# Another order of the seven block products in a feed-forward layer, a later place for half of the down-weight maxima, and two operand passes exchanged

## The chip, the cores and the metric
One core of one Trainium2 chip runs the kernel. The metric is device microseconds (us) of one execution, the median of several. TensorE (PE) does the matrix products, VectorE (DVE), ScalarE (ACT) and GpSimd (POOL) the elementwise work, and SyncE (SP) issues nearly all DMA transfers. Each engine works through its own instructions strictly in order and waits on semaphores for the others.

## The reference, cut to what matters
One layer over 2048 rows of 1024 float32 columns: four token mixers, an output projection with a norm, and a feed-forward part with 4096 hidden columns. The change lies in the last three steps:

```python
mix = jnp.concatenate([ya, yb, yc, yd], axis=-1)            # four mixers, 256 columns each
h = h + rms_norm(jnp.einsum('bsm,md->bsd', mix, w_out[layer]), norm_mix_post[layer])

u = rms_norm(h, norm_ffn_pre[layer])
f = jnp.square(jax.nn.relu(jnp.einsum('bsd,df->bsf', u, w_ff_up[layer])))
h = h + rms_norm(jnp.einsum('bsf,fd->bsd', f, w_ff_down[layer]), norm_ffn_post[layer])
```

## The kernel before
**What is multiplied.** The feed-forward products are Strassen-Winograd products of 2x2 blocks: seven products (indices 0 to 6) of sums and differences of blocks in place of eight. For accuracy each float32 operand is split into an f16 high part (a cast on ACT) and an f16 low part (a subtraction on DVE), and every product is done with three matmuls (`mm3`). The tuple `TURN` says in which order operands are made (`in_turn`), `SHELF` in which order f operands lie in DRAM.

**The up stage.** `ffn_norm` (L1593) loads rows of h (`nh`), normalises them, forms the four block differences `nt` on GpSimd with `diffs`, transposes all seven operands on PE (`fut`) and splits them into `u`. Then follow 32 blocks, `up_block(g, cp)` (L1705), for 16 pairs g of weight tiles and two halves cp of the rows. A block has seven products of 12 matmuls each. Its four PSUM accumulators X, Y, Z, V come from two rings of two banks. X takes product 0 and then 1, Y takes 5, Z takes 6 and then 3, V takes 4 and then 2. The second product of a bank is added onto the first one after DVE has read that first one: `us` is X (copied by ACT) plus Y, `c` is `us` plus Z, `c` then gets V added, and after products 3 and 2 there are further sums `c`. ACT takes relu and square of each into the tiles `e`.

`up_weights(g)` loads two raw weight tiles (`ur`), multiplies them by the norm gain on POOL, takes maxima on DVE (`a_up`, `m_up`), transposes the maxima on PE (`p_up`, in the code `p2_up`) for a scale `s_up`, forms differences `us0` to `us3` of weights on POOL and splits into `uw`. It runs two pairs ahead of the products. The names us80 to us83 are such weight differences, us60 and us61 the row sums of blocks (6,0) and (6,1).

**From up to down.** The results f of a block go to DRAM tiles `fD`. The 16 pairs are cut into six passes (`PASSES`, of 2, 2, 3, 3, 3, 3 pairs). For passes 1 to 5 `up_operands` (L1759) makes the sums `fz` on POOL and the splits `fs` at once and stores all seven operands in f16. For pass 0 `put` stores the raw float32 values, and `f_operands` (L1791) loads them in the down stage (`fr`), makes the sums `ft` on POOL and the splits `fo`.

**The down stage.** `run` (L1894) takes the passes in the order `QS` (1, 0, 2, 3, 4, 5). For each pass `down_weights` loads raw weights (`dr`), makes differences (`ds0..3`) on POOL and splits (`dw`), and eight calls of `down_block` (L1812) do seven products of 6 matmuls (passes of two pairs) or 9 matmuls each. They have the same four accumulators; the sums go into `y`, three of them on POOL (`y<-y,ds`). Before that, `down_top(x)` (L1686) has loaded the same raw weights once to take their maxima (`a_dn`) for the scale `kd`.

**The buffers that matter.** `ur` and `dr` tiles share one ring of two buffers (tag wraw): a load waits until the one before the last has been read for the last time. The down weights' temporaries and the block sum share the name `ds`.

**What sets the order.** Nearly every instruction is issued from L562 of a planner (`weave`) which merges lanes of work by due times, priorities and estimated costs into one static order for each engine. The order in which code is written inside a lane is kept. A `claim` takes a buffer early.

## Time and profile before

| what | value |
|---|---|
| median of three executions | 2643.15 us (2639.71 to 2643.21) |
| the profiled execution | 2652.18 us |
| its span in the trace | 2650.4 us |
| PE busy | 2460.2 us, 93% |
| DVE busy | 1801.0 us, 68% |
| ACT busy, POOL busy | 1261.8 us, 1180.5 us |
| mean granted PE clock | 0.971 |

In the profiled execution the out-projection ends and `ffn_norm` begins around 1200 to 1310 us, the steady up blocks run from 1431.4 to 1994.5, the down stage follows and its second pass (the raw one) lies from 2107.3 to 2201.5. A window's "PE busy" counts matmuls that run; what is missing to the window's length is time in which PE stood still. The clock column is a share of full speed.

### The profile page before, as it was taken

Reading aid. Unit: us, or ns where it says so; the run is one execution under the profiler, and the core shown is the slowest. Engines: PE = TensorE matmul, PEld = TensorE weight load, DVE = VectorE, ACT = ScalarE, POOL = GpSimd, SP = SyncE. Lnnn points to the kernel's source line nnn. Section 1 sums busy time; section 2 is a strip of 40 time slices with the busy share of each in tenths; the row PEclk is TensorE's granted clock in tenths of the full one; section 3 lists DMA queues with packets and bytes.
Section 4 is the critical chain, followed back from the end, with each engine's and each line's share of the span. In section 5 each row is a group of like instructions: output and inputs, shape, how many; then the busy total and the mean of one; then the engine's idle time right before and its main releaser. Section 6 shows DMA issues by size and latency. Waiting matters only on the chain.

```text
span 2650.4 us, 39473 instructions
## 1 busy us (share of the span) xinstructions
PE 2460.2 (93%) x14186; PEld 1299.4 (49%) x14186; DVE 1801.0 (68%) x3801; ACT 1261.8 (48%) x2563; POOL 1180.5 (45%) x1147
## 2 busy tenths in 40 slices
PE   7999999999989998987897999999997989999998
PEld 5545575656645565643444444444443434444443
DVE  6487986766788778657754677777756785445355
ACT  6377775434456676644334565565555321112022
POOL 5373331020265445444344545545534474344357
PEclk9999999999999997998897999999998999999999
DMA  6522226362351525237652333443335313333256
GB/s 185 151 72 83 83 74 186 70 182 46 87 150 50 154 83 157 85 89 244 223 164 80 96 115 115 129 129 111 124 116 193 128 48 136 120 136 135 103 190 221
DMA packets 306548, 334.33 MB, mean 126 GB/s; under 512 B 51316, under 2 KB 264244, under 8 KB 301743
## 3 DMA queue, kind: packets, MB, share of 16 engines
q1 hardware_dynamic: 306351, 331.79, 40.4%
q8 instruction: 112, 1.84, 0.3%
q14 instruction: 85, 0.70, 0.1%
HBM read 225.49 MB, written 113.06 MB: 128 GB/s over the span
## 4 chain that ended last, share of the span: by engine, by line
PE 52%; DVE 16%; POOL 10%; DMA 8%; ACT 7%; issue 6%; SPq 1%; DVEq 0%; POOLq 0%; ACTq 0%
PE mz L562 8%; PE mx L562 7%; PE mv L562 7%; PE pt L562 5%; PE po L562 4%; PE my L562 4%; DVE e L562 4%; POOL fz L562 3%; PE pv L562 2%; PE as L562 2%; ACT e L562 2%; PE do L562 2%; POOL y L562 2%; DVE fs L562 2%; PE dt L562 2%
## 5 line engine op out<-in xcount | busy, mean ns | idle before, releaser
L562 PEld LDWEIGHTS <-fo 128*128 128x128 f16 x2688 | 264.5, 98 | 362.7 <-issue 47.8
L562 PEld LDWEIGHTS <-uw 128*128 128x128 f16 x2688 | 264.3, 98 | 344.9 <-issue 39.2
L562 PE MATMUL pt<-uuh,wh 128*128 128x512 f16 x640 | 243.9, 381 | 0.1
L562 PE MATMUL pt<-uuh,wl 128*128 128x512 f16 x640 | 243.4, 380 | 0.5 <-DVE wl L562 0.5
L562 PE MATMUL pt<-uul,wh 128*128 128x512 f16 x640 | 243.5, 380 | 0.0
L562 POOL TENSOR_TENSOR y<-y,ds 128x512 f32<-128x512 f32 x112 | 147.2, 1338 | 206.9 <-DVE ds L562 206.9
L562 DVE CUSTOM_DVE_ANT_0 e<-sc,strip,scf 128x512 f32<-128x512 f32 (+3 forms) x320 | 206.1, 663 | 25.5 <-PE sc L562 16.0
L562 PE MATMUL mz<-dw,fo 128*128 128x512 f16 x768 | 185.1, 385 | 16.6 <-DVE y L562 16.3
L562 PE MATMUL mv<-u,uw 128*128 128x512 f16 x768 | 179.9, 383 | 21.9 <-DVE c L562 21.9
L562 PE MATMUL mx<-dw,fo 128*128 128x512 f16 x768 | 184.0, 381 | 16.3 <-ACT ds L562 11.7
L562 ACT ACTIVATE e<-e,dmn 128x1024 f32<-128x1024 f32 (+4 forms) x192 | 171.5, 895 | 47.3 <-DVE dmn L562 44.1
L562 PE MATMUL mv<-dw,fo 128*128 128x512 f16 x768 | 183.8, 383 | 3.1 <-DVE y L562 3.0
L562 PE MATMUL po<-woh,mx 128*128 128x512 f16 x512 | 169.2, 398 | 17.8 <-ACT mx L562 10.0
L562 PEld LDWEIGHTS <-wh 128*128 128x128 f16 x1280 | 123.1, 98 | 126.8 <-issue 22.5
L562 PE MATMUL mz<-u,uw 128*128 128x512 f16 x768 | 179.6, 380 | 3.1 <-DVE c L562 3.1
L562 PE MATMUL mx<-u,uw 128*128 128x512 f16 x768 | 180.8, 382 | 0.0
L562 POOL TENSOR_SCALAR e<-e,dcf 128x256 f32<-128x256 f32 (+4 forms) x96 | 77.4, 806 | 161.3 <-DVE dcf L562 127.5
L562 ACT ACTIVATE ae<-ae,mt 128x256 f32<-128x256 f32 (+1 forms) x192 | 87.1, 455 | 113.4 <-DVE mt L562 99.2
L562 POOL TENSOR_TENSOR ur<-ur,g_ffn 128x1024 f32<-128x1024 f32 x32 | 62.0, 1938 | 164.5 <-DMA ur<-in_w_ff_up_dram 151.0
L562 PEld LDWEIGHTS <-mx 128*128 128x128 f16 x768 | 77.4, 103 | 110.9 <-issue 13.7
L562 DVE TENSOR_TENSOR fs<-fz,fs 128x512 f16<-128x512 f32 x112 | 108.1, 1025 | 32.4 <-ACT fs L562 32.1
L562 ACT ACTIVATE ds<-mx 128x512 f32<-128x512 f32 x48 | 28.4, 591 | 202.0 <-PE mx L562 202.0
(332 smaller groups left out, 5626.1 us busy)
## 6 DMA issues: line engine op xcount, KB each, us to landing
fD<-fs SPq DMA_DIRECT2D x84, 512.0 KB, 3.0
fo<-fD SPq DMA_DIRECT2D x32, 1344.0 KB, 6.1
dr<-in_w_ff_down_dram SPq DMA_DIRECT2D x64, 512.0 KB, 4.5
ur<-in_w_ff_up_dram SPq DMA_DIRECT2D x32, 512.0 KB, 4.2
wr<-in_w_in_dram SPq DMA_DIRECT2D x24, 512.0 KB
xt<-in_x_dram SPq DMA_DIRECT2D x16, 512.0 KB, 8.0
mr<-mixT SPq DMA_DIRECT2D x16, 512.0 KB, 5.7
oxr<-in_x_dram SPq DMA_DIRECT2D x16, 512.0 KB, 4.8
```

Source lines behind the costliest of these rows:

```text
L562: op.ins.append(fn(*[real(a) for a in args], **{n: real(a) for n, a in kw.items()}))
```

## The change
There are seven edits.

1. `TURN` is (0, 5, 6, 4, 1, 3, 2), so operands are made in another order.
2. In `up_block` products run as X0, Y5, Z6, V4, X1, Z3, V2, where it was X0, Y5, X1, Z6, V4, Z3, V2. The first two blocks keep X1 before Z6. The tiles `e` are taken in the other order, and the choice between two pools for them switches from the third block on and not from the fifth.
3. `down_block` has the same new product order.
4. `QS` is (1, 2, 0, 3, 4, 5): the raw pass comes third.
5. In pass 0 only the half cp = 0 stays raw; cp = 1 is stored as ready f16 operands.
6. `ffn_norm` makes its differences on VectorE.
7. `down_top` is called for 8 of 16 pairs at the place where all 16 were; the others follow one per pair, for pairs 3 to 10 of the up weights.

```diff
@@ -31,8 +31,8 @@
 NC = -(-NB // 3)
 U = 1024.0
 UF = 256.0
-TURN = (0, 5, 1, 6, 4, 3, 2)
-QS = (1, 0, 2, 3, 4, 5)
+TURN = (0, 5, 6, 4, 1, 3, 2)
+QS = (1, 2, 0, 3, 4, 5)
 SHELF = (0, 1, 3, 2, 4, 5, 6)
 PASSES = ((0, 2), (2, 4), (4, 7), (7, 10), (10, 13), (13, 16))
 EPS = 1e-6
@@ -1605,7 +1605,7 @@
                 h.append(x)
             q = h[0][:, 0:512], h[1][:, 0:512], h[0][:, 512:D], h[1][:, 512:D]
             z = [np.tile([P, 512], F32, tag=f"at{i % 2}", name=f"nt{cp}{j}{i}")[:] for i in range(4)]
-            diffs(nc.gpsimd, *q, *z)
+            diffs(nc.vector, *q, *z)
         with nc.lane("fn", 0):
             for i, src in in_turn(*q, *z, True):
                 nc.claim(*u[i])
@@ -1633,8 +1633,8 @@
         self.k0 = k.keep.tile([P, self.pairs], F32, tag="k0", name="k0")
         self.kd = k.keep.tile([P, self.pairs], F32, tag="kd", name="kd")
 
-        self.f = [[k.dram.tile([4, P, p1 - p0, 7, 2, P] if q else [4, P, 2 * (p1 - p0), 2 * P], F16 if q else F32,
-                               tag=f"fD{q}{cp}", name=f"fD{q}{cp}") for cp in range(2)]
+        self.f = [[k.dram.tile([4, P, p1 - p0, 7, 2, P] if q + cp else [4, P, 2 * (p1 - p0), 2 * P],
+                               F16 if q + cp else F32, tag=f"fD{q}{cp}", name=f"fD{q}{cp}") for cp in range(2)]
                   for q, (p0, p1) in enumerate(PASSES)]
         self.w, self.d, self.n, self.made = {}, {}, 0, 0
 
@@ -1725,7 +1725,7 @@
 
         def put(f):
             x = 2 * (g - PASSES[q][0]) + f
-            if q == 0:
+            if q + cp == 0:
                 nc.sync.dma_start(self.f[q][cp][:, :, x, :].rearrange("j p c -> p j c"),
                                   e[f][:].rearrange("p j a t -> p j (a t)"))
         q = next(i for i, (p0, p1) in enumerate(PASSES) if p0 <= g < p1)
@@ -1734,26 +1734,32 @@
             nc.need(*u[TURN[-1]])
             s = k.fuw.tile([P, 512], F32, tag="s", name=f"us{g}{cp}", bufs=1)
             self.made += 1
-            er = self.fst if self.made > 4 and self.made % 2 else k.fuw
-            e = [er.tile([P, 4, 2, P], F32, tag="er", name=f"e{g}{cp}{f}", bufs=2) for f in range(2)]
+            er = self.fst if self.made > 2 and self.made % 2 else k.fuw
+            early = self.made <= 2
+            e = {f: er.tile([P, 4, 2, P], F32, tag="er", name=f"e{g}{cp}{f}", bufs=2) for f in ((0, 1) if early else (1, 0))}
+            if not early:
+                nc.claim(Z)
             prod(X, 0, True)
             nc.scalar.activation(s[:], X, AF.Copy)
             prod(Y, 5, True)
             nc.vector.tensor_tensor(s[:], s[:], Y, op=ALU.add)
-            prod(X, 1, False)
-            act(X, 0, 0)
-            prod(Z, 6, True)
-            c = add(Z)
-            prod(V, 4, True)
-            nc.vector.tensor_tensor(c[:], c[:], V, op=ALU.add)
-            act(c[:], 1, 1)
+            for step in (0, 1) if early else (1, 0):
+                if step:
+                    prod(Z, 6, True)
+                    c = add(Z)
+                    prod(V, 4, True)
+                    nc.vector.tensor_tensor(c[:], c[:], V, op=ALU.add)
+                    act(c[:], 1, 1)
+                else:
+                    prod(X, 1, False)
+                    act(X, 0, 0)
             prod(Z, 3, False)
             act(add(Z)[:], 1, 0)
             put(1)
             prod(V, 2, False)
             act(add(V)[:], 0, 1)
             put(0)
-        if q:
+        if q + cp:
             self.up_operands(q, g - PASSES[q][0], cp, e)
 
     def up_operands(self, q, x, cp, e):
@@ -1793,7 +1799,7 @@
         k, nc = self.k, self.k.nc
         n = PASSES[q][1] - PASSES[q][0]
         with nc.lane("fprep", 1):
-            if q:
+            if q + cp:
                 w = k.fdr.tile([P, n, 7, 2, P], F16, tag="fo", name=f"fo{q}{cp}{j}", bufs=2)
                 nc.sync.dma_start(w[:].rearrange("p n i h t -> p (n i h t)"),
                                   self.f[q][cp][j].rearrange("p n i h t -> p (n i h t)"))
@@ -1832,6 +1838,7 @@
                 nc.claim(y[ta], y[tb])
             X, Y, Z, V = self.banks(True)
             s = k.fue.tile([P, 512], F32, tag="s", name=f"ds{q}{cp}{j}", bufs=2)[:]
+            nc.claim(Z)
             prod(X, 0, True)
             nc.scalar.activation(s, X, AF.Copy)
             prod(Y, 5, True)
@@ -1839,15 +1846,15 @@
             if not first:
                 for o in (y22, y21, y12):
                     (nc.gpsimd if not last or o is not y12 else nc.vector).tensor_tensor(o, o, s, op=ALU.add)
+            prod(Z, 6, True)
+            add(y22, s if first else y22, Z)
+            prod(V, 4, True)
+            add(y22, y22, V)
             prod(X, 1, False)
             if not first:
                 add(y11, y11, X)
             else:
                 nc.scalar.activation(y11, X, AF.Copy)
-            prod(Z, 6, True)
-            add(y22, s if first else y22, Z)
-            prod(V, 4, True)
-            add(y22, y22, V)
             prod(Z, 3, False)
             add(y21, s if first else y21, Z)
             prod(V, 2, False)
@@ -1902,9 +1909,8 @@
             while ready < min(n, g + 2):
                 self.up_weights(ready, 1)
                 ready += 1
-                if ready == 2:
-                    for x in range(n):
-                        self.down_top(x)
+                for x in range(8) if ready == 2 else (ready + 5,) if 2 < ready < 11 else ():
+                    self.down_top(x)
             self.up_block(g, cp)
         self.down_scale()
         self.y = [k.fd.tile([P, D], F32, tag=f"y{t}", name=f"y{t}") for t in range(NT)]
```

Three places of the static order show what comes of it.

VectorE in block (6,0) of the up stage, before, from the sum with Y to the sum with product 3 (`a_up8` and `m_up8` are maxima of the up weights two pairs ahead, `mz`, `mv`, `my` the accumulators):

```order
L562 TENSOR_TENSOR us60_17867<-us60_17867,my_17858 128x512
L562 TENSOR_REDUCE a_up8_17871<-ur81_17833 128x1
L562 TENSOR_REDUCE m_up8_17910<-a_up8_17871 128x1
L562 TENSOR_TENSOR c60_17927<-us60_17867,mz_17899 128x512
L562 TENSOR_TENSOR fs2112_17844<-fz2113_17916,fs2112_17844 128x4x128
L562 TENSOR_TENSOR fs2114_17933<-fz2110_17873,fs2114_17933 128x4x128
L562 TENSOR_TENSOR fs2114_17933<-fz2111_17893,fs2114_17933 128x4x128
L562 TENSOR_TENSOR fs2116_17946<-fz2112_17905,fs2116_17946 128x4x128
L562 TENSOR_TENSOR c60_17927<-c60_17927,mv_17921 128x512
L562 TENSOR_REDUCE s_up8_17969<-p2_up8_17960 128x1
L562 TENSOR_SCALAR s_up8_17969<-s_up8_17969 128x1 x4
L562 TENSOR_TENSOR c60_17984<-us60_17867,mz_17899 128x512
```

After, the same place:

```order
L562 TENSOR_TENSOR us60_17899<-us60_17899,my_17894 128x512
L562 TENSOR_TENSOR kd_14591<-a_dn13_17878 128x1
L562 TENSOR_TENSOR c60_17943<-us60_17899,mz_17866 128x512
L562 TENSOR_TENSOR fs2112_17880<-fz2113_17934,fs2112_17880 128x4x128
L562 TENSOR_TENSOR fs2114_17950<-fz2110_17902,fs2114_17950 128x4x128
L562 TENSOR_TENSOR fs2114_17950<-fz2111_17914,fs2114_17950 128x4x128
L562 TENSOR_TENSOR fs2116_17961<-fz2112_17925,fs2116_17961 128x4x128
L562 TENSOR_REDUCE a_up8_17974<-ur80_17890 128x1
L562 TENSOR_TENSOR c60_17943<-c60_17943,mv_17939 128x512
L562 TENSOR_REDUCE a_up8_17974<-ur81_17923 128x1
L562 TENSOR_REDUCE m_up8_18001<-a_up8_17974 128x1
L562 TENSOR_TENSOR c60_18014<-us60_17899,mz_17866 128x512
```

Both maxima stood ahead of the sum with Z and now come behind the four splits, one of them ahead of the sum with V; the maximum's scale `s_up8` leaves this block for the next.

SP's DMA issues of the same pair, before (`fD` are stores of f operands):

```order
L562 DMA fD20_17362<-fs2104_17743 128x4x512
L562 DMA fD20_17362<-fs2106_17754 128x4x256
L562 DMA ur80_17783<-in_w_ff_up_dram 128x8x128
L562 DMA ur81_17833<-in_w_ff_up_dram 128x8x128
L562 DMA fD21_17529<-fs2110_17800 128x4x512
L562 DMA fD21_17529<-fs2112_17844 128x4x512
L562 DMA fD21_17529<-fs2114_17933 128x4x512
L562 DMA fD21_17529<-fs2116_17946 128x4x256
L562 DMA fD20_17362<-fs2200_17989 128x4x512
```

After:

```order
L562 DMA dr130_17838<-in_w_ff_down_dram 128x1024
L562 DMA dr131_17863<-in_w_ff_down_dram 128x1024
L562 DMA ur80_17890<-in_w_ff_up_dram 128x8x128
L562 DMA fD21_17562<-fs2110_17851 128x4x512
L562 DMA ur81_17923<-in_w_ff_up_dram 128x8x128
L562 DMA fD21_17562<-fs2112_17880 128x4x512
L562 DMA fD21_17562<-fs2114_17950 128x4x512
L562 DMA fD21_17562<-fs2116_17961 128x4x256
L562 DMA fD20_17392<-fs2200_18016 128x4x512
```

The two loads of raw down weights now go ahead of the two of up weights through the same two buffers.

GpSimd at the passage from up to down, before, from the last sum of block (15,1):

```order
L562 TENSOR_TENSOR fz5213_20948<-e1511_20871,fz5211_20931 128x512
L562 TENSOR_TENSOR ft000_21032<-fr000_20978 128x256
L562 TENSOR_TENSOR ft000_21042<-ft000_21032,fr000_20978 128x256
L562 TENSOR_TENSOR ds30_21048<-dr30_20993 128x512
L562 TENSOR_TENSOR ft000_21061<-fr000_20978 128x256
L562 TENSOR_TENSOR ds31_21067<-dr31_21020,ds30_21048 128x512
L562 TENSOR_TENSOR ds32_21078<-dr31_21020,dr30_20993 128x512
L562 TENSOR_TENSOR ds33_21088<-dr31_21020,ds31_21067 128x512
L562 TENSOR_TENSOR ft000_21107<-fr000_20978,ft000_21042 128x256
L562 TENSOR_TENSOR ds00_21136<-dr00_21096 128x512
L562 TENSOR_TENSOR ds01_21164<-dr01_21144,ds00_21136 128x512
L562 TENSOR_TENSOR fz5200_21166<-e1500_21012,e1501_21059 128x512
```

After:

```order
L562 TENSOR_TENSOR fz5213_21005<-e1511_20913,fz5211_20988 128x512
L562 TENSOR_TENSOR ds30_21084<-dr30_21038 128x512
L562 TENSOR_TENSOR ds31_21108<-dr31_21073,ds30_21084 128x512
L562 TENSOR_TENSOR ds32_21117<-dr31_21073,dr30_21038 128x512
L562 TENSOR_TENSOR ds33_21128<-dr31_21073,ds31_21108 128x512
L562 TENSOR_TENSOR ds40_21178<-dr40_21138 128x512
L562 TENSOR_TENSOR ds41_21209<-dr41_21188,ds40_21178 128x512
L562 TENSOR_TENSOR fz5200_21212<-e1500_21130,e1501_21115 128x512
L562 TENSOR_TENSOR ds42_21214<-dr41_21188,dr40_21138 128x512
L562 TENSOR_TENSOR fz5201_21216<-fz5200_21212,e1500_21130 128x512
L562 TENSOR_TENSOR fz5202_21218<-e1500_21130 128x512
L562 TENSOR_TENSOR fz5203_21220<-e1501_21115,fz5201_21216 128x512
```

The raw operand's sums `ft000` are gone from here, and the weights of pair 4 stand where those of pair 0 were.

On PE a steady block before was cut by the next one: X0, Y5, X1, Z6, V4, three matmuls of the next block's X0, Z3, V2, and the rest of that X0. After, each block is unbroken. The passes run 1, 2, 0, 3, 4, 5; the sums `ft` are made for four blocks of pass 0 where they were made for eight. The transposes `p_up` of the pair two ahead stood in the middle of Z3 of block (g,0); now they stand behind nine matmuls of X0 of block (g,1) for pairs 7 to 10, and in Z3 of (g,0) from pair 11 on.

## Rows read from the trace of the kernel before

**Rows 1.** The page: busy time, share and instructions of each engine, and one DMA group.
```profile
PE 2460.2 (93%) x14186; PEld 1299.4 (49%) x14186; DVE 1801.0 (68%) x3801; ACT 1261.8 (48%) x2563; POOL 1180.5 (45%) x1147
...
dr<-in_w_ff_down_dram SPq DMA_DIRECT2D x64, 512.0 KB, 4.5
```

**Rows 2.** Windows: start:end, length, busy time (instructions) by engine, PE clock, DMA share, GB/s.
```profile
1200.00:1250.00 50.00, 37.45 (x173) 18.75 (x172) 34.80 (x51) 18.33 (x31) 22.48 (x24) 0.86 0.75 254
1400.00:1450.00 50.00, 36.66 (x165) 21.36 (x163) 22.81 (x31) 24.78 (x44) 20.62 (x23) 0.73 0.21 64
1750.00:1800.00 50.00, 46.85 (x218) 21.39 (x217) 37.20 (x51) 26.28 (x45) 31.62 (x22) 1.00 0.34 110
2000.00:2050.00 50.00, 33.96 (x139) 14.18 (x137) 34.52 (x45) 24.66 (x42) 23.08 (x19) 0.83 0.59 203
2107.30:2201.50 94.20, 78.22 (x337) 33.83 (x336) 81.11 (x112) 29.52 (x73) 65.61 (x57) 0.95 0.21 65
2201.50:2295.70 94.20, 94.20 (x438) 42.78 (x437) 37.17 (x52) 8.37 (x14) 36.21 (x29) 1.00 0.33 120
```

**Rows 3.** Waits, stretch 1440 to 1990: engine <- releaser: us in total, times, longest.
```profile
PE mv L562 <- DVE c L562: 21.3, 11, 2.6
```

**Rows 4.** Timeline of PE in one up pair: start, us, out<-in, [idle before <-releaser].
```profile
1754.48 2.75 PE L562 MATMUL mv<-u,uw 128*128 128x512 f16 x12
...
1761.94 2.75 PE L562 MATMUL mv<-u,uw 128*128 128x512 f16 x12 [1.89 <-DVE c L562]
```

**Rows 5.** Timeline of DVE in the same pair and at the next block.
```profile
1751.29 1.21 DVE L562 TENSOR_REDUCE a_up<-ur 128x1 f32<-128x1024 f32 x1
1754.68 0.69 DVE L562 TENSOR_TENSOR c<-us,mz 128x512 f32<-128x512 f32 x1 [2.00 <-PE mz L562]
1755.29 6.00 DVE L562 TENSOR_TENSOR fs<-fz,fs 128x512 f16<-128x512 f32 x4
1761.21 0.68 DVE L562 TENSOR_TENSOR c<-c,mv 128x512 f32<-128x512 f32 x1
...
1773.91 2.50 DVE L562 TENSOR_TENSOR fs<-fz,fs 128x512 f16<-128x512 f32 x4 [1.82 <-ACT fs L562]
```

**Rows 6.** Timeline of POOL in the same pair.
```profile
1748.86 1.90 POOL L562 TENSOR_TENSOR ur<-ur,g_ffn 128x1024 f32<-128x1024 f32 x1
...
1757.34 1.73 POOL L562 TENSOR_TENSOR us<-ur,ur 128x512 f32<-128x512 f32 x1
```

**Rows 7.** Timeline of SP's DMA issues, the loads of one pair's up weights.
```profile
1738.15 6.14 SPq L562 DMA_DIRECT2D ur<-in_w_ff_up_dram  x2
```

**Rows 8.** Waits of SP's queue, stretch 1150 to 1310 (out-projection).
```profile
SPq L562 <- DVE a_dn L562: 35.6, 19, 4.3
```

**Rows 9.** Timeline of PE in the second half of ffn_norm.
```profile
1412.06 1.11 PE L562 MATMUL fut<-ident,nt 128*128 128x128 f32 x4 [4.10 <-POOL nt L562]
```

**Rows 10.** Timeline of POOL in the same stretch.
```profile
1409.40 1.26 POOL L562 TENSOR_TENSOR nt<-nh,nh 128x512 f32<-128x512 f32 x1
```

**Rows 11.** Timeline of PE between the up and the down stage.
```profile
2007.52 1.46 PE L562 MATMUL mx<-dw,fo 128*128 128x512 f16 x3 [4.44 <-DMA fo<-fD]
...
2039.82 1.44 PE L562 MATMUL mx<-dw,fo 128*128 128x512 f16 x3 [11.38 <-ACT ds L562]
2041.05 2.77 PE L562 MATMUL mz<-dw,fo 128*128 128x512 f16 x6
```

**Rows 12.** Timeline of POOL in the same stretch.
```profile
2011.07 0.72 POOL L562 TENSOR_TENSOR ft<-fr 128x256 f32<-128x256 f32 x1 [8.66 <-DMA fr<-fD]
...
2029.21 1.26 POOL L562 TENSOR_TENSOR ds<-dr,ds 128x512 f32<-128x512 f32 x1 [6.28 <-DMA dr<-in_w_ff_down_dram]
```

**Rows 13.** Waits of PE in the pass with raw operands, 2104 to 2203.
```profile
PE mz L562 <- DVE y L562: 16.1, 6, 4.8
```

**Rows 14.** Groups on POOL, 2107 to 2201: shapes, count, busy us, mean ns, idle before.
```profile
L562 POOL TENSOR_TENSOR y<-y,ds 128x512 f32<-128x512 f32 x24 | 34.0, 1441 | 20.3 <-DVE ds L562 20.3
L562 POOL TENSOR_TENSOR ft<-fr 128x256 f32<-128x256 f32 x12 | 10.4, 871 | 5.9 <-DVE fo L562 3.9 <-issue 1.2 <-POOL ds L562 0.7
```

## The prediction

> **What bounds the kernel now.** I read the busy times first. PE is busy for 2460.2 of 2650.4 us, DVE for 68% [rows 1], so a change that neither adds nor takes away a matmul can win only where PE stands still or runs at a low clock. The windows show where [rows 2]: in the steady up stage PE works 46.85 of 50 us, in the out-projection 37.45, in `ffn_norm` 36.66 at a granted clock of 0.73, at the passage from up to down 33.96 at 0.83, and in the raw pass 78.22 of 94.2 at 0.95. The pass after that one has no loss at all, 94.20 of 94.20. From its 438 matmuls one takes 94.2/438 = 0.215 us, a product of 12 takes 2.58 and one of 6 takes 1.29.
>
> Next I read who ends these waits. In the up stage V2 waits for the sum `c` on DVE, 21.3 us in 11 waits [rows 3]. One of them can be followed [rows 4, 5]: DVE forms `c` from Z at 1754.68, then runs four splits `fs` for 6.00 us, and only at 1761.21 comes to `c` plus V, though V4, begun at 1754.48, was long over. V2 waits 1.89 us for that. The same four splits take 2.50 us in the next block [rows 5]. The longer group ran while POOL made the up weights' sums `us` [rows 6].
>
> **The change part by part**
>
> *Up blocks.* No matmul is added. With Z6, V4, X1, Z3, V2 three products, 3 x 2.58 = 7.74 us, lie between the end of Z6 and the start of V2; before there were V4, three matmuls of the next X0, and Z3, 5.8 us. That is 1.9 us more, about what one wait costs (21.3/11 = 1.94). But DVE's order now puts a maximum `a_up`, 1.21 us [rows 5], between the splits and `c` plus V. From the end of Z6 DVE needs 0.61 (start of `c` to start of the splits), 6.00, 1.21 and 0.68 = 8.5 us with the long splits, 5.0 us with the short ones. So 0.8 us of wait is left with the long splits and none with the short. What runs on POOL beside them is now mostly the products `ur` of 1.90 us [rows 6] and no longer the sums, so I can't exclude the long ones. Bounds: 21.3 - 11 x 0.8 = 12.5 and 21.3, somewhat wider for the untouched first blocks and for slow-clock products after a wait: 10 to 22. I take the middle, **-17**.
>
> What is moved onto this stage: 16 maxima `a_dn` in eight pairs. The trace shows an equal reduction, `a_up`, at 1.21 us [rows 5], so DVE gets 2.4 us more in each of these pairs. DVE is busy 37.2 of 50 us here [rows 2]; with 2.4 per 38.8 us it comes to some 81%. I cost this at nothing, because it lies beside PE's 36 us of products, and the cover is gone if the maxima stand before a sum that PE waits for. Their loads go through the two buffers ahead of `ur`; that is a rival below.
>
> *Out-projection and ffn_norm.* 16 of 32 loads and maxima leave this stage. SP, which is in order and also issues the loads `mr` and `nh`, waited 35.6 us for `a_dn` [rows 8]. Half of that is 17.8. Not all of it reaches PE, since PE's idle time is 12.55 in a window of 50 [rows 2]; ends 0 and -14, +2 if other loads merely queue in another way. I take a third of the half, **-6**. The block differences go from POOL (1.26 us [rows 10]) to DVE, where a subtraction of the same shape takes 0.62 (2.50/4 [rows 5]). PE waits for the first two, up to 4.10 us [rows 9], so about 2 x 0.64 = 1.3 us per block of rows is won twice in the second half. Against that, `TURN` now makes operand 1 the fifth and not the third one; that is the operand that frees the first `nh` buffer, and the next load waits for two more transposes of some 1.1 us and a split each. I take **0**, with -3 and +3 as ends.
>
> *Passage to down.* PE waits 4.44 us for the first f load and 11.38 for `ds`, and works at half clock for one product after it (2.77 us for six matmuls) [rows 11]. The first wait stays: the load still follows the last sum of block (15,1). The second comes from POOL and the weight loads: POOL waited 8.66 us for the raw operand, made its sums (0.72 us for one) amid the weight differences, and then waited 6.28 us for the next raw weights [rows 12]. The raw operand is gone from here, and Z6 and V4 of the second down block, 2 x 1.29 us, now stand ahead of the product that waited. The weights' load chain itself, 4.5 us a load [rows 1], stays. I expect 11.4 to shrink to some 6: **-5**, ends -10 and +1.
>
> *Raw pass.* Its 56 products would need 56 x 1.29 = 72.3 us and take 94.2: 21.9 are lost, 16.0 as idle time and the rest at the lower clock [rows 2]. The waits are Z3 for `y` plus Z6 on DVE, 16.1 us in 6 [rows 13]. DVE is there 81.1 of 94.2 us busy [rows 2]. Two things change. Four of eight blocks come as ready operands, without sums `ft` (0.87 us each) and splits; and in all blocks V4 and X1 now lie between Z6 and Z3, 1.29 us more slack. Half of the loss goes with the four blocks (11); of the other half, three waits of 2.7 us shrink by 1.3 each (4). **-15**. Ends: -22 (nothing is lost any more) and -8 (only the half, and the weights of the pass with three pairs, which are now due one pass earlier, cost 3). POOL's sums into `y`, 1.44 us each and 20.3 us of waiting for `ds` in front [rows 14], must be over before `y` plus Z6; that sum now comes 1.29 us sooner after Y5, which is the cost of the new order here. It is covered by the longer time to Z3.
>
> *Extra work.* Two more operand sets are formed in the up stage for pass 0, those of blocks (0,1) and (1,1), in place of raw stores. All later blocks do the same beside PE: 0, up to +3.
>
> **Sum.** -6 + 0 - 17 - 5 - 15 = -43. Against the profiled execution's 2652.2 this is 2609.2. The median of the runs, 2643.15, lies 9 us lower, so the time to compare is 2643.15 - 43 = **2600**. The best ends together give -71 (2572), the worst +2 + 3 - 10 + 1 - 8 + 3 = -9 (2634).
>
> **The rivals**
>
> *The wait in the up stage stays.* DVE gains the maxima and `a_up` in front of `c` plus V; the slack gained is 1.9, the work put in front 1.2, and when `a_up` itself has to wait for its weights, the sum behind it waits too. Then the 17 are gone and 26 remain: 2617, or up to 2632 if the raw blocks also keep their waits. For it speak the 6.00 us of long splits; against it that the short ones leave 2.7 us to spare.
>
> *Up weights late (the slower side).* The raw weights share two buffers. Before, SP issued both `ur` of a pair within 6.14 us [rows 7]. Now two loads `dr` of 4.5 us with their maxima go ahead in eight pairs, so `ur` comes some 6 us later. By my count the second one is on chip 10 us after the block's start, its product and its maximum are done by 16 to 17, and PE asks for `p_up` at 18.1 + 1.9 = 20: 3 to 4 us to spare. If the chain is longer, PE, being in order, stands at `p_up`, and the next loads are late too. It decides from 43/8 = 5.4 us of wait per pair; with 8 us the time is 2643 - 43 + 64 = 2664. For it speaks that SP stands behind each `dr` with the stores `fD`; against it the DMA share of 0.34 in this stage [rows 2].
>
> *The lock.* The splits beside POOL were slower by 0.87 us each ((6.00 - 2.50)/4) [rows 5]. If each of the four had to wait for a whole POOL product of 1.90 us [rows 6], they would take 4 x (0.62 + 1.90) = 10.1, `c` plus V would end 12.6 us after Z6, and V2 would wait 4.9 us in place of 1.94: +32 in place of -17, and the time is 2643 + 6 = 2649. The trace so far speaks against a full wait per split. In the Trainium skill, "SBUF — State Buffer", section "Who interferes with whom", this is a rule: a VectorE instruction with two SBUF inputs and a GpSimd instruction that reads SBUF take turns at one port for a whole instruction. The trace agrees in that both slow down (a sum on POOL takes 1.73 us there [rows 6] and 1.26 with DVE quiet [rows 10]), not in the full size.
>
> *No effect.* The planner's waits just move to the next sum; within 0.2%.
>
> **How the numbers follow.** The forecast gets 0.62 (2572 to 2611), the kept wait 0.24 (2611 to 2634), no effect 0.05, late up weights 0.06, the lock 0.03. The range from 2576 to 2633 leaves out the last three and a little of the first. 0.2% of this time is 5 us, about what a measurement can tell from no change. Faster 0.86, same 0.05, slower 0.09.
>
> **What would show it.** Right: waits of V2 for `c` under 8 us in all; PE over 48.5 of 50 us in the steady windows; no wait at `p_up`; a second wait at the passage near 6 us; a raw pass, now third of the passes, of about 79 us. Wrong: waits of PE at `p_up` or of DVE's maxima for `ur` (late weights), splits `fs` of over 8 us for four (the lock), or a raw pass still above 88 us.

## The result, and the profile after

The changed kernel takes 2655.04 us (median of 6 runs, 2651.45 to 2660.38), the kernel before 2642.16 beside it. The medians differ by 12.9 us. The ratio of the runs is 1.0056 with an interval of 1.0035 to 1.0076: slower by 0.56%, where 43 us less were forecast and 2633 was the top of the range.

The two profiled spans are nearly equal, 2650.4 us before and 2650.9 after. That is a matter of the one execution of before: it took 2652.2 us where the median is 2642. So a second trace of the kernel before was taken (the run `before_again`), and stages are compared rather than spans. The borders of the stages are read from PE's timeline: the start of the first product of block (0,1), the first matmul of the down stage, the end of the last matmul.

| run | (0,1) starts at | up stage | down stage | after the last matmul |
|---|---|---|---|---|
| before | 1431.4 | 576.1 | 633.7 | 9.2 |
| before, second trace | 1424.9 | 570.1 | 632.9 | 9.1 |
| after | 1425.1 | 589.3 | 625.2 | 11.3 |

So the change gains 8 us in the down stage, pays 2 of them back behind it, and loses 13 to 19 us in the up stage, which was to give 17. In the up stage that is idle time of PE and slow matmuls and nothing else: less PE's waits and less what its matmuls take beyond their usual 0.2155 us, the stage takes 541 to 542 us in the traces of before, of after and of all runs below. What stood ahead of the up stage differs by 6.5 us between two traces of the same kernel, and after lies within that.

The page after, its first line. DVE has 26 us more to do than in [rows 1]:

```profile
PE 2465.7 (93%) x14186; PEld 1301.5 (49%) x14186; DVE 1826.9 (69%) x3819; ACT 1256.1 (47%) x2549; POOL 1142.5 (43%) x1107
```

Windows of after, with the columns of [rows 2]:

```profile
1650.00:1700.00 50.00, 46.36 (x201) 20.69 (x201) 39.39 (x58) 29.74 (x52) 24.14 (x17) 0.93 0.41 130
1750.00:1800.00 50.00, 49.86 (x233) 22.75 (x232) 40.72 (x53) 30.87 (x54) 25.82 (x17) 1.00 0.43 138
2222.90:2307.40 84.50, 75.10 (x337) 33.32 (x336) 64.64 (x89) 24.74 (x50) 56.04 (x44) 0.96 0.29 104
```

The same first window in the trace of before:

```profile
1650.00:1700.00 50.00, 48.02 (x224) 21.78 (x223) 34.99 (x51) 29.99 (x53) 26.73 (x18) 1.00 0.37 121
```

The first line is a window of the up stage's first half: PE is busy for 46.4 of 50 us at a granted clock of 0.93, where before it was busy for 48.0 at 1.00. (0.93 is a mixture of the two levels, 2.4 and 1.2 GHz.) The second, the window of [rows 2] at 1750, is nearly full now: the last late maximum began at 1719.5. The last is the raw pass: 75.1 busy of 84.5, where 78.2 of 94.2 were.

Waits of PE for the sums c in the stretch of [rows 3]:

```profile
PE mv L562 <- DVE c L562: 20.3, 9, 3.9
PE mz L562 <- DVE c L562: 11.1, 3, 3.9
```

V2 (mv) waits for 20.3 us, as before, in fewer and longer waits; Z3 (mz) has 11.1 us in three waits, where both traces of before have 3.1 us, none over 0.6.

One wait of V2, DVE's timeline, the place in an earlier pair that [rows 5] show before:

```profile
1639.55 0.68 DVE L562 TENSOR_TENSOR c<-us,mz 128x512 f32<-128x512 f32 x1
1641.53 7.36 DVE L562 TENSOR_TENSOR fs<-fz,fs 128x512 f16<-128x512 f32 x4 [1.31 <-ACT fs L562]
1648.82 1.21 DVE L562 TENSOR_REDUCE a_up<-ur 128x1 f32<-128x1024 f32 x1
1649.94 0.67 DVE L562 TENSOR_TENSOR c<-c,mv 128x512 f32<-128x512 f32 x1
```

The second of the four splits by itself:

```profile
1643.16 2.38 DVE L562 TENSOR_TENSOR fs<-fz,fs 128x512 f16<-128x512 f32 x1
```

GpSimd beside it, the second product `ur` and the first sum `us`:

```profile
1642.65 2.34 POOL L562 TENSOR_TENSOR ur<-ur,g_ffn 128x1024 f32<-128x1024 f32 x1
1645.07 1.60 POOL L562 TENSOR_TENSOR us<-ur 128x512 f32<-128x512 f32 x1
```

And PE, with a later wait for comparison:

```profile
1650.67 4.24 PE L562 MATMUL mv<-u,uw 128*128 128x512 f16 x12 [3.94 <-DVE c L562]
...
1828.28 2.75 PE L562 MATMUL mv<-u,uw 128*128 128x512 f16 x12 [1.59 <-DVE c L562]
```

The clock while that product ran (window columns as above):

```profile
1651.80:1655.10 3.30, 3.30 (x9) 1.10 (x8) 1.57 (x4) 3.17 (x7) 0.00 (x0) 0.50 0.00 0
```

The reader is to see three things. The four splits take 7.36 us, where they took 6.00 in [rows 5] and 2.50 when GpSimd was quiet. One by one they take 1.71, 2.38, 1.76 and 1.75 us: the first begins inside the first product ur, the second runs beside the second product (2.34 us, 1.90 in [rows 6]), the last two beside the sums us. Behind them stands the maximum a_up, and only then c plus V. And the wait of 3.94 us is followed by a product that takes 4.24 us and not 2.75, with a granted clock of 0.50 (1.2 GHz) for most of it, while after the wait of 1.59 us the product takes 2.75. The long waits cost twice, once as idle time and once at the lower clock.

Four of V2's waits (2.86, 3.94, 2.97 and 2.94 us) look like this one. The three waits of Z3 (3.62, 3.87 and 3.56 us) do not. Here the splits fs are short, and what makes c late is the up weights' own work on VectorE, the splits `uw`:

```profile
1580.59 2.42 DVE L562 SCALAR_TENSOR_TENSOR uw<-us,s_up,uw 128x512 f16<-128x512 f32 x2
1582.92 2.49 DVE L562 TENSOR_TENSOR fs<-fz,fs 128x512 f16<-128x512 f32 x4
...
1585.99 0.68 DVE L562 TENSOR_TENSOR c<-us,mz 128x512 f32<-128x512 f32 x1
```

```profile
1586.72 4.44 PE L562 MATMUL mz<-u,uw 128*128 128x512 f16 x12 [3.56 <-DVE c L562]
```

### The profile page after: what moved, and what is told of

Its sections match the earlier page's. It is cut to its first block, busy times and chain, and to the rows that moved or that the text cites. A ratio compares the mean times of both kernels' runs of the same rounds, so it can differ in the third digit from the quotient of the medians.

```text
span 2650.9 us, 39441 instructions
## 1 busy us (share of the span) xinstructions
PE 2465.7 (93%) x14186; PEld 1301.5 (49%) x14186; DVE 1826.9 (69%) x3819; ACT 1256.1 (47%) x2549; POOL 1142.5 (43%) x1107
## 4 chain that ended last, share of the span: by engine, by line
PE 51%; DVE 18%; POOL 11%; DMA 7%; ACT 7%; issue 5%; SPq 1%; DVEq 0%; POOLq 0%; ACTq 0%
PE mv L562 8%; PE mz L562 7%; PE mx L562 7%; PE pt L562 6%; DVE e L562 4%; PE my L562 3%; PE po L562 3%; DVE fs L562 3%; POOL fz L562 3%; ACT e L562 3%; PE as L562 2%; PE do L562 2%; POOL y L562 2%; PE pv L562 2%; PE dt L562 2%
## 5 line engine op out<-in xcount | busy, mean ns | idle before, releaser
L562 PE MATMUL mv<-u,uw 128*128 128x512 f16 x768 | 184.5, 390 | 20.4 <-DVE c L562 20.3
L562 PE MATMUL mx<-dw,fo 128*128 128x512 f16 x768 | 184.1, 383 | 13.6 <-ACT ds L562 7.0
L562 PE MATMUL mz<-u,uw 128*128 128x512 f16 x768 | 184.4, 389 | 11.1 <-DVE c L562 11.1
L562 DVE TENSOR_TENSOR fs<-fz,fs 128x512 f16<-128x512 f32 x120 | 124.1, 1093 | 33.1 <-ACT fs L562 32.4
L562 POOL TENSOR_TENSOR fz<-e,e 128x512 f32<-128x512 f32 x30 | 41.4, 1380 | 201.3 <-ACT e L562 199.2
```

The costliest lines, as they stand in the source:

```text
L562: op.ins.append(fn(*[real(a) for a in args], **{n: real(a) for n, a in kw.items()}))
```

## The experiments

The edits are numbered as in the change: 1 `TURN`, 2 up blocks, 3 down blocks, 4 pass order, 5 half the raw pass ready, 6 differences on VectorE, 7 later maxima. Beside each group of runs the kernel before took 2639.5 to 2641.4 us.

### Which edit costs

**Edit 7 undone.** All 32 maxima are in the out-projection again; the rest of the change stays.

```diff
-                for x in range(8) if ready == 2 else (ready + 5,) if 2 < ready < 11 else ():
-                    self.down_top(x)
+                if ready == 2:
+                    for x in range(n):
+                        self.down_top(x)
```

> The changed kernel with one edit undone: all 32 loads and maxima of the down weights stand again in the out-projection (edits 1 to 6 stay). Theory A (the later maxima are the cause: their loads go ahead of the up weights through two buffers, push the ur products and a_up beside and behind the four splits fs, and so c plus V and V2 come late): the up stage loses its waits of 3 to 4 us and its slow-clock products, about 30 us back, while the out-projection gives up the 6 us it had gained, so 2615 to 2632 us, and V2 waits for c are under 8 us in all. Rival B (the new order of the seven products in the up blocks is the cause by itself): the waits of 3 to 4 us stay, 2645 to 2660 us.

Measured: 2635.92 us, ratio 0.9984 (0.9970 to 0.9998). The up stage is 573.5 us. So the later maxima cost about 19 us of the changed kernel (2655 to 2636); theory A holds in its direction and B falls, though 2635.9 lies above A's range. But only 4 us below before are left of six edits, and V2 still waits 16 us where A had under 8. That was not expected by either.

**Edit 7 alone**, put into the kernel before (the diff above, the other way round).

> The kernel before with the later maxima alone (edit 7). Theory A: the out-projection gains 6 us and the up stage loses 10 to 20, so 2645 to 2662 us, with splits fs of over 7 us for four beside the ur products. Rival B: only the gain is seen, 2632 to 2640 us.

Measured: 2661.25 us, ratio 1.0079 (1.0066 to 1.0093). The up stage is 587.4 us, 11 to 17 more than before. And nothing is gained ahead of it: block (0,1) starts at 1426.3 us, between the two traces of before. In this kernel, too, every second group of four splits lasts 6.1 to 7.4 us, most of them 6.8, with a_up between them and c plus V.

**What in edit 7 costs.** The maxima of the later eight pairs over 8 columns and not 1024; the loads and the ring of two buffers stay.

```diff
-                nc.vector.tensor_reduce(a[:, f:f + 1], raw[f][:], axis=AX.X, op=ALU.max, apply_absolute_value=True)
+                nc.vector.tensor_reduce(a[:, f:f + 1], raw[f][:, 0:8] if g >= 8 else raw[f][:], axis=AX.X, op=ALU.max, apply_absolute_value=True)
```

> The kernel before with the later maxima (edit 7), where the maxima of pairs 8 to 15 are taken over 8 columns and not 1024, so their value is not the right one; the loads and the ring are the same. If VectorE's time for them is the cost (2 x 1.1 us in eight pairs, 18 us), the time is 2640 to 2648 us. If the place that the ring gives to the up weights is the cost, a_up and c plus V stand as in the run with the full maxima, and the time stays at 2652 to 2662 us.

Measured: 2658.39 us, ratio 1.0071 (1.0049 to 1.0093), against 1.0079 with full maxima. Its group of maxima on DVE, 1440 to 1760 (count, busy us, mean ns, idle before):

```profile
L562 DVE TENSOR_REDUCE a_dn<-dr 128x1 f32<-128x8 f32 x16 | 2.4, 152 | 3.5 <-DMA dr<-in_w_ff_down_dram 3.4
```

DVE's timeline at a late c plus V:

```profile
1687.78 6.75 DVE L562 TENSOR_TENSOR fs<-fz,fs 128x512 f16<-128x512 f32 x4 [0.76 <-ACT fs L562]
1694.46 1.21 DVE L562 TENSOR_REDUCE a_up<-ur 128x1 f32<-128x1024 f32 x1
1695.59 0.67 DVE L562 TENSOR_TENSOR c<-c,mv 128x512 f32<-128x512 f32 x1
```

17 us of VectorE's time are gone (16 x 1.06), and the kernel takes as long. So it is not the maxima's own time that costs; by elimination it is the place: the loads dr go through the ring ahead of ur, the products ur and the maxima a_up of the up weights come at a time when the splits run, and c plus V stands behind all of it. SP's waits in after, 1440 to 1760, show the ring at work, as many waits for `a_dn` as there are late maxima, where before has none:

```profile
SPq L562 <- DVE a_dn L562: 32.9, 16, 3.0
```

A ring of their own for these loads was not tried. SP issues all loads in order, so a load that waits holds back the ones behind it as well; the runs do not tell that apart from the two buffers.

### Why the new block order gains so little

**Edits 1 and 2 alone**, in the kernel before.

```diff
-TURN = (0, 5, 1, 6, 4, 3, 2)
+TURN = (0, 5, 6, 4, 1, 3, 2)
```

and the hunk of `up_block`.

> The kernel before with the new product order in the up blocks and TURN alone (edits 1 and 2). Theory A: DVE forms c plus V ahead of the splits, the waits of V2 (21 us before) nearly go, 2618 to 2632 us. Rival B: 2645 to 2660 us, with waits of V2 for c of over 25 us in all.

Measured: 2639.21 us, ratio 0.9993 (0.9979 to 1.0007), no change. Neither theory had that. The up stage is 562 us, 8 to 14 less, but block (0,1) starts at 1430.9, 6 us later than in the second trace of before, and in the up stage V2 still waits for 17.1 us in 11 waits. Some of the later start belongs to the edit: the end of the norm, from the last matmul of the out-projection (`po`) to block (0,1), takes 57.8 us here, against 53.6 or 53.7 in the eight traces with the old `TURN`. Where V2's waits come from is seen in DVE's timeline of one pair:

```profile
1745.48 0.69 DVE L562 TENSOR_TENSOR c<-c,mv 128x512 f32<-128x512 f32 x1
1746.30 6.15 DVE L562 TENSOR_TENSOR fs<-fz,fs 128x512 f16<-128x512 f32 x4
...
1753.32 0.68 DVE L562 TENSOR_TENSOR c<-us,mz 128x512 f32<-128x512 f32 x1
...
1764.32 2.49 DVE L562 TENSOR_TENSOR fs<-fz,fs 128x512 f16<-128x512 f32 x4 [2.45 <-ACT fs L562]
...
1768.06 0.68 DVE L562 TENSOR_TENSOR c<-c,mv 128x512 f32<-128x512 f32 x1
```

PE in the second block of that pair:

```profile
1768.79 2.75 PE L562 MATMUL mv<-u,uw 128*128 128x512 f16 x12 [1.81 <-DVE c L562]
```

In the first block c plus V (1745.48) now stands ahead of the splits, as theory A expected, and V2 does not wait. But the splits beside GpSimd's sums still take 6.15 us, so the sum with Z3 (1753.32) is late, and with it the tiles e, the sums fz and the next splits. In the second block c plus V stands behind these (1768.06), and V2 waits 1.81 us there. The wait was moved by one block.

**The sums us on VectorE for every pair.** If the splits are long because GpSimd works beside them, then giving VectorE GpSimd's four sums should make it quicker.

```diff
-            sums(nc.gpsimd, *q, *z)
+            sums(nc.vector, *q, *z)
```

Once in the kernel before, once with edits 1 to 6:

> The kernel before with the sums us on VectorE alone. Theory L: the splits fall to 2.5 us, V2's waits of 1.9 us go, 2620 to 2632 us. Rival W: 2641 to 2660 us.

> The kernel without the later maxima (edits 1 to 6), with the up weights' four sums us formed on VectorE and not on GpSimd. Theory L (the four splits fs last 6.2 us and not 2.5 because GpSimd's sums run beside them; what the new order saves at one V2 is lost at the next): with GpSimd quiet there the splits take 2.5 us, DVE does 2.5 us more and 3.6 us less per pair, the waits of V2 for c fall from 16 us to under 6, the up stage is 10 to 18 us shorter, 2618 to 2627 us. Rival W (VectorE simply has too much to do): 2.5 us more per pair on VectorE, waits of V2 grow, 2636 to 2655 us.

Measured: 2641.27 us, ratio 0.9993 (0.9977 to 1.0009), and 2648.16 us, ratio 1.0024 (1.0012 to 1.0037). By the totals theory L is refuted; by the stages it is not. The up stage is 549.7 and 553.2 us, 20 to 26 less than in the kernel before and 20 less than with edits 1 to 6. But block (0,1) starts at 1447.9 and 1452.9, some 20 to 30 us late: the sums of the first three pairs fall ahead of it, and the planner's order there came out otherwise. So the two were taken apart.

**The same from pair 3 on**, which leaves the order ahead of the up stage as it was:

```diff
-            sums(nc.gpsimd, *q, *z)
+            sums(nc.vector if g >= 3 else nc.gpsimd, *q, *z)
```

> The kernel before with the sums us on VectorE for pairs 3 to 15 only, so that the order up to the up stage stays as it was. Theory L (the splits are long because GpSimd's sums run beside them, and the 20 us that the earlier run won in the up stage were lost ahead of it by another order of the first two pairs): the up stage falls from 570 to about 552 us and nothing is given back, 2618 to 2626 us. Rival W (the gain is tied to what was lost before it): 2636 to 2642 us.

Measured: 2621.07 us, ratio 0.9926 (0.9909 to 0.9944). This one edit gains 20 us, in the kernel before and with its old block order. The up stage is 547.4 us. V2's waits there, 1440 to 1970:

```profile
PE mv L562 <- DVE c L562: 0.6, 1, 0.6
```

19 to 21 us of waits of V2 are 0.6 now. VectorE's groups in the up stage of the second trace of before, and GpSimd's four sums there:

```profile
L562 DVE TENSOR_TENSOR fs<-fz,fs 128x512 f16<-128x512 f32 x106 | 103.0, 1031 | 26.8 <-ACT fs L562 26.8
```

```profile
L562 POOL TENSOR_TENSOR us<-ur,ur 128x512 f32<-128x512 f32 x13 | 21.4, 1647 | 0.0
L562 POOL TENSOR_TENSOR us<-ur,us 128x512 f32<-128x512 f32 x13 | 21.4, 1643 | 0.0
L562 POOL TENSOR_TENSOR us<-us,ur 128x512 f32<-128x512 f32 x13 | 20.7, 1590 | 1.0
L562 POOL TENSOR_TENSOR us<-ur 128x512 f32<-128x512 f32 x13 | 16.6, 1273 | 0.2
```

VectorE in the up stage of this run:

```profile
L562 DVE TENSOR_TENSOR fs<-fz,fs 128x512 f16<-128x512 f32 x106 | 66.2, 686 | 9.0 <-ACT fs L562 8.6
L562 DVE TENSOR_TENSOR us<-us,ur 128x512 f32<-128x512 f32 x13 | 9.0, 692 | 0.5
L562 DVE TENSOR_TENSOR us<-ur,ur 128x512 f32<-128x512 f32 x13 | 8.9, 683 | 0.0
L562 DVE TENSOR_TENSOR us<-ur,us 128x512 f32<-128x512 f32 x13 | 8.9, 682 | 0.0
L562 DVE TENSOR_TENSOR us<-ur 128x512 f32<-128x512 f32 x13 | 8.9, 682 | 0.0
```

106 splits took 103.0 us and take 66.2; the 52 sums, 80 us on GpSimd, take 35.7 on VectorE. Together VectorE spends 101.9 us where it spent 103.0. The work moved onto the busier engine cost that engine nothing. In the second trace of before 61 of the 106 splits run with GpSimd quiet and take 0.69 us each; the others overlap with the sums us and take 1.5 on average.

**The second trace of before:**

> The kernel before once more, for a second trace, since the first one (2652.2 us) lies above the median of its timed runs (2641 us). Both theories: the steady up pairs show the same V2 waits of 1.9 us; the 10 us of difference lie in the stages ahead of the feed-forward part, so the up stage is 576 us long again (from X0 of block (0,1) to the first matmul of the down stage) and the down stage 634.

It is the second row of the first table: the up stage is 6 us shorter than in the first trace, not equal as expected: the first trace has 2.2 us more of V2's waits (21.3 and 19.1) and 3.5 us more of products at the lower clock (4.5 and 1.0). Another 6.5 us lie ahead of it.

**The whole change with it**, and the change without edit 7:

> The whole change, all seven edits, with the sums us on VectorE for pairs 3 to 15. Theory L: the splits beside GpSimd's sums and products were what made the later maxima costly; the up stage falls from 589 to 555 to 570 us, 2620 to 2638 us. Rival (the maxima and their loads cost on their own, by the ring of two buffers): the up stage stays above 575 us, 2640 to 2655 us.

> Edits 1 to 6, without the later maxima, with the sums us on VectorE for pairs 3 to 15. Theory L: the up stage falls from 573 to about 555 us, the down stage keeps its 624, 2612 to 2622 us, the fastest so far. Rival W: 2634 to 2640 us.

Measured: 2653.15 us, ratio 1.0042 (1.0027 to 1.0058), and 2613.9 us, ratio 0.9900 (0.9882 to 0.9917). With the later maxima nothing is won (the up stage is 588.1 us), as the rival had it and against theory L; without them the gain is there. DVE's timeline of the whole change with the sums on VectorE:

```profile
1649.04 5.22 DVE L562 TENSOR_TENSOR fs<-fz,fs 128x512 f16<-128x512 f32 x4 [1.31 <-ACT fs L562]
1654.18 1.20 DVE L562 TENSOR_REDUCE a_up<-ur 128x1 f32<-128x1024 f32 x1
1655.31 0.67 DVE L562 TENSOR_TENSOR c<-c,mv 128x512 f32<-128x512 f32 x1
```

In this place the splits still take 5.22 us, since the two products ur are still on GpSimd beside them, and a_up still stands ahead of c plus V. But that wait of V2 is 2.3 us, and the longest one comes elsewhere and without contention:

```profile
1542.92 2.50 DVE L562 TENSOR_TENSOR fs<-fz,fs 128x512 f16<-128x512 f32 x4 [1.82 <-ACT fs L562]
...
1551.12 0.68 DVE L562 TENSOR_TENSOR c<-c,mv 128x512 f32<-128x512 f32 x1
```

```profile
1551.85 5.28 PE L562 MATMUL mv<-u,uw 128*128 128x512 f16 x12 [7.72 <-DVE c L562]
```

Between the two rows of VectorE stand three of the four sums us and six splits uw, all of the late up weights. So what edit 7 costs is the up weights' work coming late on both engines, and the contention is one part of it. Edit 7 costs 39 us here, twice what it cost in the kernel before.

**A price for the planner alone.** The order is set by estimated costs. Here the splits are reckoned at 1.5 us and not 0.6; edits 1 to 6, no instruction changed.

```diff
+        if name == "tensor_tensor" and n == 512 and self.thread.lane == "fform":
+            return 1.5, 0
```

> The kernel without the later maxima (edits 1 to 6), where the planner alone reckons each split fs at 1.5 us and not at 0.6 when it sets the order; no instruction is changed. Theory L: c plus V then stands ahead of the splits in more blocks, V2's waits shrink, but the splits themselves stay at 6 us and come later, so the sums after them do too: 2625 to 2636 us. Rival W: no change, 2633 to 2640 us.

Measured: 2682.89 us, ratio 1.0155 (1.0135 to 1.0176), far outside both. V2 waits 41.9 us in 20 waits:

```profile
PE mv L564 <- DVE c L564: 41.9, 20, 3.4
```

A price that is nearer to what contention makes of a split gave a worse order. Why the planner came to it wasn't followed up.

### The down stage and the norm

**Edits 4 and 5 alone:** the pass order and the ready half, as in the change.

```diff
-QS = (1, 0, 2, 3, 4, 5)
+QS = (1, 2, 0, 3, 4, 5)
...
-        if q:
+        if q + cp:
             self.up_operands(q, g - PASSES[q][0], cp, e)
```

> The kernel before with the passes exchanged and half of the raw pass stored as ready operands (edits 4 and 5). Both theories: these edits gain in the down stage, 5 to 12 us, so 2630 to 2638 us. If this run is 2642 or more, the trace's shorter raw pass (9.4 us of waits in place of 16.1) is paid for elsewhere in the down stage.

Measured: 2641.95 us, ratio 1.0007 (0.9996 to 1.0017). The down stage is 622.9 us, 10 to 11 less, as expected. The up stage is 581.8, 6 to 12 more, and that is where it goes: two more operand sets are formed there. Block by block the run is 14.5 us behind the second trace of before at the fourth block from (0,1) on, and 11.7 at the end. Waits of PE, 1440 to 1990:

```profile
PE mx L562 <- ACT us L562: 14.4, 21, 2.9
PE mz L562 <- DVE c L562: 6.6, 12, 3.0
PE mv L562 <- DVE c L562: 4.1, 1, 4.1
```

The longest lie at 1462 to 1493 us, about where the extra sets are made (4.1, 3.0 and 2.9 us). The rest, most of them waits of X0 of 0.1 to 1.0 us for ACT's copy us, which before had none, stand in place of V2's waits of before and lose nothing against them.

**The same with the sums us on VectorE:**

> Edits 4 and 5 (exchanged passes, half the raw pass ready) with the sums us on VectorE for pairs 3 to 15. If the 11 us of the down stage were eaten by the extra operand sets in an up stage already short of VectorE time, they show now: 2608 to 2614 us against 2621 with the sums alone. If the extra sets cost as much whatever else runs: 2617 to 2623 us.

Measured: 2622.31 us, ratio 0.9934 (0.9912 to 0.9955), against 0.9926 without the two edits. The down stage is 621.7 us and the up stage 562.2, 15 more than without them. The second expectation holds: the extra sets cost as much as the raw pass gains, whether or not GpSimd's sums contend.

**Edit 3 left out** (edits 1, 2, 4, 5, 6 and the sums on VectorE), and **edits 3 and 6 left out**; each leaves the hunk of `down_block` as before, the second also this line:

```diff
-            diffs(nc.vector, *q, *z)
+            diffs(nc.gpsimd, *q, *z)
```

> The same without edit 3 (the old product order in the down blocks): PE's last matmul is followed by 9 us and not by 11, since y11 is summed early again; the raw pass loses a few us more. Within 3 us of the run with edit 3, 2610 to 2624 us.

> Edits 1, 2, 4 and 5 with the sums us on VectorE for pairs 3 to 15, so the norm's differences stay on GpSimd. PE waited 13 us for them on GpSimd and 18 us on VectorE with the new TURN, so edit 6 is worth -3 to +3 us: 2607 to 2614 us against 2610.7 with it.

Measured: 2610.73 us, ratio 0.9884 (0.9866 to 0.9902), and 2619.51 us, ratio 0.9917 (0.9890 to 0.9943). The first has the lowest time of this study; against the same kernel with edit 3 (2613.9 us) the intervals overlap. Its last matmul is followed by 9.1 us, with edit 3 by 11.3, as in after. The second lies above its expected 2607 to 2614. By the two ratios edit 6 gains some 9 us (0.3%), but the intervals overlap at 0.989 to 0.990, and block (0,1) starts anywhere from 1421.1 to 1431.8 in kernels that are alike up to there (no_late_tops, six_us_late), so the 10 us between 1426.5 and 1436.9 are not all its own. The end of the norm, from the last matmul of the out-projection to block (0,1), differs far less from trace to trace: 53.6 or 53.7 us in the eight traces with the old `TURN`, 57.7 and 57.8 in the two with the new `TURN` and the differences on GpSimd, 54.2 to 54.7 in the seven with the differences on VectorE too. There the new `TURN` costs 4 us, and edit 6 gives 3 of them back.

| run | (0,1) starts at | up stage | down stage | after the last matmul | ratio |
|---|---|---|---|---|---|
| no_late_tops | 1421.1 | 573.5 | 623.9 | 11.3 | 0.9984 |
| late_tops_only | 1426.3 | 587.4 | 632.7 | 9.1 | 1.0079 |
| late_thin | 1434.9 | 587.1 | 632.7 | 9.1 | 1.0071 |
| up_block_only | 1430.9 | 562.2 | 633.9 | 9.2 | 0.9993 |
| passes_only | 1425.8 | 581.8 | 622.9 | 9.1 | 1.0007 |
| before_us_late | 1427.5 | 547.4 | 633.8 | 9.1 | 0.9926 |
| p45_us_late | 1422.8 | 562.2 | 621.7 | 9.4 | 0.9934 |
| six_us_late | 1431.8 | 553.5 | 623.5 | 11.3 | 0.9900 |
| five_us_late | 1426.5 | 553.4 | 619.7 | 9.1 | 0.9884 |
| four_us_late | 1436.9 | 553.7 | 620.2 | 9.1 | 0.9917 |
| after_us_late | 1426.5 | 588.1 | 623.0 | 11.3 | 1.0042 |

## Why the prediction was wrong, step by step

**The up blocks, -17: wrong, +13 to +19.** By the up stages of the runs, edits 1 and 2 alone take it from 570 to 576 us down to 562, edits 3 to 6 up to 573.5 (by passes_only that is the extra operand sets), the later maxima up to 589.3.

The step that failed is the sum for c plus V, "0.61, 6.00, 1.21 and 0.68 = 8.5 us with the long splits". The order was read rightly; the term 6.00 was taken from a place where GpSimd did other work. With the products ur beside them the splits take 7.36 us, so the sum of the row times is 9.86 us from c to the end of c plus V. That is 2.1 us more than the 7.74 of slack, and waiting for ACT's split, 1.31 us, comes on top. The prediction saw that ur would run there and even said that it could not exclude the long splits, yet it took 6.00 as their upper end.

The reason lies one step earlier, in "slower by 0.87 us each" and "the trace so far speaks against a full wait per split". 0.87 is a mean over the merged row of four. One by one the splits of [rows 5] take 0.94, 1.79, 1.75 and 1.75 us; one of them:

```profile
1757.87 1.75 DVE L562 TENSOR_TENSOR fs<-fz,fs 128x512 f16<-128x512 f32 x1
```

Three of four were slower by 1.1, nearly as long as a whole sum of 1.27 on GpSimd. Read so, the trace spoke for the rule that was set aside, and a split beside a product of 1.90 could be put at up to 0.62 + 1.90 = 2.52 us; 2.38 was measured.

The sum also knows only the splits fs ahead of c. The three waits of Z3, 11.1 us, stand behind the splits uw of the late up weights, a term that it doesn't have. (Without the later maxima, in no_late_tops, one wait of Z3 of 4.4 us is left.) And it left out that a wait of 3 to 4 us costs a second time at the lower clock: what the up stage's products of 12 matmuls take beyond 2.75 us adds up to 13.1 us in PE's timeline, against 4.5 and 1.0 in the two traces of before.

The slack that it counted is real but was worth less than counted: edits 1 and 2 alone shorten the up stage by 8 to 14 us and not 17, since V2's wait moves by one block. (A small slip in it: the block whose V2 waits in [rows 4], cp = 0, is not the one that the next X0 cuts. In it V4, Z3 and two transposes p_up lie there, 5.6 us, so 2.2 us of slack were gained and not 1.9.)

**The maxima "at nothing": wrong, some 19 us.** Their own time did cost nothing that shows (late_thin). The cover named, PE's 36 us of products, was not what counted; their loads decided what came first in the two buffers.

**The rivals.** The lock had the chance 0.03 and gave 2649; it came nearest, with 2655 measured, and that is partly luck. Its rule came out nearly in full for the one split that ran beside a whole product, but it put all four beside products (10.1 us), where two of them ran beside the shorter sums (7.4). It expected V2 to wait longer in all 11 pairs, where V2's total stayed at 20.3 us, and it had neither the waits of Z3 nor the lower clock nor the extra sets. The late up weights (0.06) had the right cause, the loads dr ahead of ur in the ring, and the wrong place: there is no wait of PE at `p_up` in after. The two belong together: the ring moves ur, ur meets the splits fs, and the splits uw come late as well. Taken apart they looked unlikely; together they had 0.09 of slower.

**Out-projection, -6: not shown.** Half the maxima and loads left, and (0,1) starts at 1425.1 to 1434.9 in the four kernels with edit 7 where before has 1424.9 and 1431.4. From the first to the last matmul of the out-projection it is 314 us in after and 319 in the other three, against 317 to 324 without edit 7. No gain from half of SP's waiting time [rows 8] is seen at PE.

**ffn_norm, 0: right, +1, as far as the end of the norm shows it.** There the new `TURN` costs 4.1 us, more than the worse end of +3, and the differences on VectorE give 3.0 to 3.6 back.

**Passage, -5: half right, -2.** The first wait stayed (3.55 us) and the second fell to 7.0, where 6 was said [rows 11]. A third, of 3.1 us for another f load, had not been foreseen, so the three add up to 13.6 us where two were 15.8:

```profile
2014.42 1.46 PE L562 MATMUL mx<-dw,fo 128*128 128x512 f16 x3 [3.55 <-DMA fo<-fD]
...
2045.91 1.44 PE L562 MATMUL mx<-dw,fo 128*128 128x512 f16 x3 [7.01 <-ACT ds L562]
...
2058.18 2.74 PE L562 MATMUL mx<-dw,fo 128*128 128x512 f16 x6 [3.08 <-DMA fo<-fD]
```

The main reason that was given, the raw operand gone from GpSimd, did not shorten the second wait. In passes_only it is gone too, with the old product order, and the wait is as long as before:

```profile
2040.14 1.44 PE L562 MATMUL mx<-dw,fo 128*128 128x512 f16 x3 [11.90 <-ACT ds L562]
```

**Raw pass, -15: too much, -10.** It takes 84.5 us and not 94.2; 79 was said. The waits of [rows 13] fell from 16.1 to 9.4 us:

```profile
PE mz L562 <- DVE y L562: 9.4, 4, 5.8
```

One wait of 5.8 us is longer than any before, and the three waits that were to shrink by 1.3 each did not do so as a group. Nor does edit 3 show a gain in the runs: without it (five_us_late) the down stage is 619.7 us, with it (six_us_late) 623.5.

**Extra operand sets, "0, up to +3": wrong, 6 to 15 us.** That all later blocks form such sets beside PE was taken as a reason. In the first blocks they do not fit beside PE: passes_only has lost 14.5 us by the fourth block.

**The tail**, not in the sum: 2 us, since the sum y11, first in the last block's finish, now comes after Z6 and V4.

## What to carry to other kernels

Read the price of a VectorE instruction with both inputs in SBUF by what GpSimd does beside it, one instruction at a time and not by the mean of a merged row, and when a change moves GpSimd's work, price the instruction anew at its new neighbour. Work given back from GpSimd to a VectorE that is already at 75% can be free, if it takes the contention away. When loads of several kinds share a ring, a load put in early moves everything that follows in that ring, whatever its own cost; and after a change that gains in one stage, look at the next block and the stage ahead before adding the gain up.

## What the runs showed of the hardware

A subtraction of 512 columns on VectorE with both inputs in SBUF takes 0.62 us alone (four in 2.50). Beside a GpSimd sum of 512 columns it takes 1.75, and the sum 1.71 in place of 1.27; beside a GpSimd product of 1024 columns it takes 2.38, and the product 2.34 in place of 1.90. An instruction of a single column shows it most clearly. In the up stage of before VectorE's product k of two single columns takes 0.14 to 0.16 us nine times and 1.89 four times:

```profile
1748.88 1.89 DVE L562 TENSOR_TENSOR k<-c 128x1 f32<-128x1 f32 x1
```

This one began 0.02 us after the GpSimd product ur of 1.90 in [rows 6], and ended with it. The Trainium skill, "SBUF — State Buffer", section "SBUF: two separate sides", says that such a VectorE instruction and a GpSimd instruction that reads SBUF hold a shared pair of ports in turn, each for a whole instruction. The trace agrees: a whole turn each would give 0.62 + 1.27 = 1.89 and 0.62 + 1.90 = 2.52 us for a split, some 0.14 us more than measured.

A wait of 1.6 to 1.9 us left the next product at 2.75 us in the rows above, at a granted clock of 1.00 (2.4 GHz); one of 3.9 us was followed by a product of 4.24, most of it at 0.50 (1.2 GHz).
